# The way down of two ConvFFNs as a Strassen product with the inner tiles in three parts

## The chip, the core and the metric

The kernel runs on one core of one Trainium2 chip. The metric is the device time of one execution in microseconds, taken as the median of several. A core has five engines with queues of their own: TensorE (PE in the rows; PEld is its weight load), VectorE (DVE), ScalarE (ACT), GpSimd (POOL) and SyncE (SP), which here starts the DMA loads. Each engine takes its instructions in order; semaphores tie the engines together.

## The reference

The input is x, 512 positions of 1024 channels in float32. Two layers run one after the other, first a mixer of pooling and block-sparse attention, then a recurrent block, each followed by the same gated ConvFFN with its own weights, and each step adds to the residual:

```python
def conv_ffn(h, w_in, conv_w, conv_b, w_out):
    z = causal_dwconv(h @ w_in, conv_w, conv_b)
    u, g = jnp.split(z, 2, axis=-1)
    return (jax.nn.gelu(g) * u) @ w_out

for l in range(DEPTH):
    x = x + mixer(rms_norm(x, norm_mix[l]))
    x = x + conv_ffn(rms_norm(x, norm_ffn[l]), ...)
```

The inner width is 2816, 22 tiles of 128 channels; `w_in` has 44 such tiles of columns (22 for u, 22 for g), and `w_out` is 2816 x 1024, a product of 22 inner tiles with 8 output tiles.

## The kernel before

Channels lie on partitions and the 512 positions along a row: X[d], d = 0 to 7, are the residual's tiles of 128 x 512. Every product is made of three matmuls (`mm3`, L223 to L226): each float32 operand is split into a high part, a cast that ScalarE makes, and a low part, the rest, that VectorE subtracts. High by high, high by low and low by high are summed in PSUM. A matmul has a 128 x 128 weight tile and up to 512 columns of the moving operand.

All weights come in one list, `chunks`, in the order of use. `load` (L175) starts a chunk's DMA into one of three `wraw` buffers on SP's queue; `convert` (L183) makes `whi` on ScalarE (L195) and `wlo` on VectorE (L196) in one of four pairs of buffers; `wnext` (L199) hands out the next pair and keeps three conversions ahead. A load waits until a `wraw` buffer has been converted, a conversion until TensorE is done with a `whi` and `wlo`.

A ConvFFN (`ffn`) runs in two halves of 11 inner tiles. In the way up of a half, an up tile `up` of g and one of u (24 matmuls each) follow each other; `conv` takes each from PSUM as `z` (VectorE, L700), makes `a` on ScalarE (L702) and adds the two shifted taps on VectorE (L704). g goes through ScalarE's GeLU (`gg`), y = u * gg is VectorE's (L718), and its high and low parts `yy` are kept (L230, L231). In the way down (`down`) each of the 8 output tiles `dn` sums the half's 11 inner tiles (33 matmuls of 512 columns) and VectorE adds it to X[d] (L312). In the last half `after` then makes the next norm's split and sum of squares of X[d] (`Norm.tile_done`: `xh` on ScalarE, `xl` on VectorE, L234, and `ss` on GpSimd, L260), or stores it; the very last tile is done in two halves of 256 columns. The order on each engine is a scheduler's, made when the program is built; where `pe["on"]` is set, TensorE keeps the order of the code.

Of the kernel before, what the change touches and what calls it, by code (L numbers as in the profile page):

```python
# [17 lines left out]
P = 128  # L18
S = 512
# [49 lines left out]

@with_exitstack  # L70
def tile_trunk(ctx: ExitStack, tc: tile.TileContext, xT, par, fpar, w_v, w_q, w_k, w_u, w_pool, w_po, w_ao,
# [63 lines left out]
    chunks = []  # L135
    for src in (w_q, w_k):
        chunks += [(src[i], 1024) for i in range(4)]
    for what in MIX_ORDER:
        if what == "v":
            chunks += [(w_v[i], 1024) for i in range(4)]  # L140
        elif what[0] in "uf":
            chunks.append((w_u[int(what[1])], 1024))
        elif what == "a":
            chunks.append((w_pool, 4 * P))
            chunks += [(w_po[i], 1024) for i in range(4)]
    chunks += [(w_ao[i], 1024) for i in range(4)]

    def ffn_chunks(w_in, w_out):
        for h in range(2):
            for j in range(h * NF // 2, (h + 1) * NF // 2):  # L150
                chunks.extend([(w_in[NF + j], 1024), (w_in[j], 1024)])
            for d in range(KD):
                chunks.extend([(w_out[h][d][:, :6 * P], 6 * P), (w_out[h][d][:, 6 * P:], 5 * P)])

    ffn_chunks(f0_in, f0_out)
    for kind, n in RG_ORDER:
        if kind == "x":
            chunks.append((r_in[RB + n], 1024))
        elif kind == "p":
            if n % 2 == 0:  # L160
                chunks.append((r_ax[n // 2], 4 * P))
        elif kind == "g":
            chunks.append((r_in[n], 1024))
    for d in range(KD):
        chunks.extend([(r_out[d][:, :5 * P], 5 * P), (r_out[d][:, 5 * P:], 5 * P)])
# [16 lines left out]

    def convert():  # L183
        n = chunks[len(ready)][1]
        if len(raws) == len(ready):
            load()
        raw = raws[len(ready)]
# [4 lines left out]
        parts = 2 if len(ready) < 2 else 2 if pe["on"] and len(ready) in FINE else 1  # L192
        for i in range(parts):
            c = slice(i * n // parts, (i + 1) * n // parts)
            nc.scalar.copy(hi[:, c], raw[:, c])  # L195
            nc.vector.tensor_tensor(lo[:, c], raw[:, c], f(hi[:, c]), op=ALU.subtract)  # L196
        ready.append((hi, lo, n))

    def wnext(n, ahead=AHEAD):  # L199
        while len(ready) < min(used[0] + 1 + ahead, len(chunks)):  # L200
            convert()
        hi, lo, got = ready[used[0]]
        assert got == n
        used[0] += 1
        return hi, lo
# [93 lines left out]
    def down(parts, yh, yl, after, cuts=None):  # L299
        nk = len(yh)  # L300
        for d in range(KD):
            w = [wnext(n * P) for n in parts]
            spans = cuts if cuts and d == KD - 1 else [slice(0, S)]
            for t in spans:
                ps = MM("dn")
                k = 0
                for n, (wh, wl) in zip(parts, w):
                    for i in range(n):
                        c = slice(i * P, (i + 1) * P)
                        mm3(ps[:, t], wh[:, c], wl[:, c], yh[k][:, t], yl[k][:, t], k == 0, k == nk - 1)  # L310
                        k += 1
                nc.vector.tensor_tensor(X[d][:, t], ps[:, t], X[d][:, t], op=ALU.add)  # L312
                if len(spans) > 1:
                    after(d, t)
            if len(spans) == 1:
                after(d)
# [376 lines left out]
    def ffn(layer, norm, after, cuts=None):  # L693
# [13 lines left out]
        for h0 in range(2):  # L707
            half(h0 * NF // 2, conv, after if h0 else (lambda d: None), cuts if h0 else None)

    def half(j0, conv, after, cuts):  # L710
        yh, yl = [], []
        for j in range(j0, j0 + NF // 2):
            g = conv(NF + j)
            gg = T("gg")
            nc.scalar.activation(gg, g, AF.Gelu_apprx_tanh)  # L715
            u = conv(j)
            y = T("y")
            nc.vector.tensor_tensor(y, u, gg, op=ALU.mult)  # L718
            hi, lo = split_of(y, None, T("yy", F32R), T("yy", F32R))
# [110 lines left out]
    phase("ffn1", z=4, a=4, gg=2, y=2, yy=30)  # L830
# [4 lines left out]
    ffn(1, nf1, store, [slice(0, S // 2), slice(S // 2, S)])  # L835
# [15 lines left out]
def _two(w):  # L851
    return np.stack([_lhs(w[:FF // 2], KD), _lhs(w[FF // 2:], KD)])
# [11 lines left out]
def _layout(i):  # L864
# [9 lines left out]
    for l in range(2):  # L874
# [32 lines left out]
```

## Time and profile before

| | us |
|---|---|
| three runs, median (lowest to highest) | 1100.43 (1099.63 to 1101.14) |
| the profiled execution | 1099.4 |
| its span, first to last instruction | 1097.6 |
| TensorE busy | 1081.9 |
| VectorE busy | 724.6 |
| ScalarE busy | 514.2 |
| GpSimd busy | 93.1 |

The profile shows one execution. Busy times are sums of an engine's instructions; TensorE's matmuls overlap in a pipeline, so the cost of one is read from the distance of starts and not from its own length. The granted clock of TensorE is given as a share of 2.4 GHz; its mean here is 0.998.

### The profile page before, as it was taken

The page shows a single profiled execution, that of the slowest core. Times are in us where ns is not written, and L with a number is a line of the kernel's source. Part 1 is how long each engine was busy: PE and PEld are TensorE (multiplying, and loading weights), DVE is VectorE, ACT ScalarE, POOL GpSimd, SP SyncE. Part 2 cuts the span into 40 slices and gives each one's busy share as a digit, 9 for nine tenths or more (in the row PEclk, how much of TensorE's full clock was granted, in tenths as well). Part 3 has the DMA queues.
Part 4 walks back from the last instruction along what each step waited for, and adds up shares of the span by engine and source line. Part 5 has one row for each costly group of instructions (what it writes and reads, how often), then busy time and mean ns, then how long its engine had stood idle before and what let it go on. Part 6 is the DMA issues. An engine that isn't in the chain of part 4 may idle for free.

```text
span 1097.6 us, 12782 instructions
## 1 busy us (share of the span) xinstructions
PE 1081.9 (99%) x4895; PEld 891.6 (81%) x4895; DVE 724.6 (66%) x1013; ACT 514.2 (47%) x749; POOL 93.1 (8%) x76
## 2 busy tenths in 40 slices
PE   8999999999999999999999898999999999999998
PEld 6888877888888888888888676888888888888887
DVE  7778877877743577764486969448777435777631
ACT  6557766444422344433448694354444223444420
POOL 5031003000000000001103332120000000000000
PEclk9999999999999999999999999999999999999999
DMA  6332112222233322223323131343332333332241
GB/s 223 131 92 91 58 47 89 97 96 96 67 89 113 116 96 96 84 71 103 118 96 106 48 102 56 102 145 96 96 96 67 91 111 115 96 96 84 78 134 51
DMA packets 35261, 105.40 MB, mean 96 GB/s; under 512 B 4096, under 2 KB 4992, under 8 KB 35200
## 3 DMA queue, kind: packets, MB, share of 16 engines
q1 hardware_dynamic: 34416, 103.48, 29.7%
q10 hardware_dynamic: 784, 1.11, 0.4%
q8 instruction: 38, 0.62, 0.2%
q14 instruction: 23, 0.19, 0.1%
HBM read 101.43 MB, written 2.10 MB: 94 GB/s over the span
## 4 chain that ended last, share of the span: by engine, by line
PE 90%; DVE 6%; ACT 3%; issue 1%; DMA 0%; POOL 0%; SPq 0%; DVEq 0%; ACTq 0%; POOLq 0%
PE up L218 44%; PE dn L218 26%; PE tk L218 5%; PE xr L218 2%; PE gt L218 2%; PE po L218 2%; PE u L218 2%; PE ao L218 2%; DVE h L783 1%; PE gp L218 1%; PE s L218 1%; DVE wlo L196 1%; DVE h L781 1%; PE av L218 1%; PE tr L221 1%
## 5 line engine op out<-in xcount | busy, mean ns | idle before, releaser
L195 ACT CAST whi<-wraw 128x1024 fp32r<-128x1024 f32 (+3 forms) x225 | 202.7, 904 | 278.9 <-PE dn L218 154.2
L196 DVE TENSOR_TENSOR wlo<-wraw,whi 128x1024 fp32r<-128x1024 f32 (+3 forms) x225 | 237.9, 1060 | 112.8 <-ACT whi L195 110.2
L218 PE MATMUL up<-xl,whi 128*128 128x512 f32 x704 | 274.0, 389 | 0.0
L218 PE MATMUL up<-xh,whi 128*128 128x512 f32 x704 | 273.9, 389 | 0.0
L218 PE MATMUL up<-xh,wlo 128*128 128x512 f32 x704 | 273.9, 389 | 0.0
L218 PE MATMUL dn<-yy,whi 128*128 128x512 f32 (+1 forms) x886 | 268.1, 384 | 2.4 <-ACT yy L230 2.0
L218 PEld LDWEIGHTS dn<-yy,whi 128*128 128x128 f32 x886 | 165.0, 188 | 36.7 <-ACT yy L230 2.8
L218 PE MATMUL dn<-yy,wlo 128*128 128x512 f32 (+1 forms) x443 | 170.0, 384 | 0.0
L218 PEld LDWEIGHTS up<-xl,whi 128*128 128x128 f32 x704 | 132.2, 188 | 28.0 <-DVE xl L234 0.5
L218 PEld LDWEIGHTS up<-xh,whi 128*128 128x128 f32 x704 | 132.2, 188 | 27.4
L218 PEld LDWEIGHTS up<-xh,wlo 128*128 128x128 f32 x704 | 132.2, 188 | 27.3
L704 DVE SCALAR_TENSOR_TENSOR a<-z,fprm,a 128x510 f32<-128x510 f32 (+1 forms) x176 | 131.0, 747 | 4.2 <-ACT a L702 0.8
L700 DVE TENSOR_TENSOR z<-up,rbc 128x512 f32<-128x512 f32 x88 | 60.5, 688 | 89.3 <-PE up L218 89.2
L218 PEld LDWEIGHTS dn<-yy,wlo 128*128 128x128 f32 x443 | 83.2, 188 | 16.2
L260 POOL TENSOR_TENSOR ss<-ss,sq 128x512 f32<-128x512 f32 x28 | 40.9, 1462 | 488.3 <-ACT sq L259 487.8
L230 ACT CAST yy<-y 128x512 fp32r<-128x512 f32 x44 | 27.3, 621 | 112.1 <-DVE y L718 112.1
L312 DVE TENSOR_TENSOR x<-dn,x 128x512 f32<-128x512 f32 (+1 forms) x41 | 27.8, 678 | 73.8 <-PE dn L218 73.7
L702 ACT ACTIVATE a<-z,fprm 128x512 f32<-128x512 f32 x88 | 71.4, 813 | 3.8 <-DVE z L700 3.2
L715 ACT ACTIVATE gg<-a 128x512 f32<-128x512 f32 x44 | 27.8, 632 | 80.8 <-DVE a L704 80.8
L231 DVE TENSOR_TENSOR yy<-y,yy 128x512 fp32r<-128x512 f32 x44 | 30.4, 692 | 28.8 <-ACT yy L230 28.8
L218 PE MATMUL tk<-wlo,xh 128*128 128x512 f32 x96 | 37.6, 392 | 2.0 <-DVE wlo L196 2.0
L218 PE MATMUL tk<-whi,xh 128*128 128x512 f32 x96 | 38.0, 401 | 0.5 <-ACT whi L195 0.5
(186 smaller groups left out, 1229.0 us busy)
## 6 DMA issues: line engine op xcount, KB each, us to landing
wraw<-in_dram SPq DMA_DIRECT2D x131, 512.0 KB, 3.3
wraw<-in_dram SPq DMA_DIRECT2D x48, 320.0 KB, 2.9
wraw<-in_dram SPq DMA_DIRECT2D x32, 384.0 KB, 3.1
x<-in_dram SPq DMA_DIRECT2D x8, 256.0 KB, 5.7
out_dram<-x SPq DMA_DIRECT2D x7, 256.0 KB, 2.0
wraw<-in_dram SPq DMA_DIRECT2D x6, 256.0 KB, 2.7
qka<-qka ACTq DMA_DIRECT2D x8, 128.0 KB, 2.3
wraw<-in_dram SPq DMA_DIRECT2D x4, 128.0 KB, 3.4
```

What stands on the lines that cost most here:

```text
L195: nc.scalar.copy(hi[:, c], raw[:, c])
L196: nc.vector.tensor_tensor(lo[:, c], raw[:, c], f(hi[:, c]), op=ALU.subtract)
L218: in_order(nc.tensor.matmul(*a, **k))
L221: in_order(nc.tensor.transpose(*a))
L230: nc.scalar.copy(hi, src)
L231: nc.vector.tensor_sub(lo, src, f(hi))
L260: nc.gpsimd.tensor_tensor(self.ss, self.ss, sq, op=ALU.add)
L312: nc.vector.tensor_tensor(X[d][:, t], ps[:, t], X[d][:, t], op=ALU.add)
L700: nc.vector.tensor_tensor(z, ps, bc, op=ALU.mult)
L702: nc.scalar.activation(a, z, AF.Identity, scale=cw[2], bias=cw[3])
L704: nc.vector.scalar_tensor_tensor(a[:, sh:], z[:, :S - sh], w, a[:, sh:], op0=ALU.mult, op1=ALU.add)
L715: nc.scalar.activation(gg, g, AF.Gelu_apprx_tanh)
```

## The change

Each way down is now a product of blocks by Strassen's scheme in Winograd's form: seven block products take the place of eight. One block is a pair of output tiles (d, d+1) by half of the part's inner tiles by half of the positions (Q = 256). The inner tiles come in three parts, of 8, 8 and 6, in place of two of 11, so a layer has three ways up and three ways down.

On the weights' side of a pair of output tiles stand `a` (the first tile's row of weights, products 1 and 2), `b` (the second half of the second tile's, product 4), `s` (two sums, products 5 and 6) and `r` (two more, products 3 and 7). GpSimd makes `ws` and `wr` by four additions of half a chunk; they are split as other weights are. On the inner side, two inner tiles y give four blocks, and three or four differences `tt` of these (t1, t3, t2, t4) are made by GpSimd, for a part's last two tiles by VectorE; the seven blocks that the products take are split into `yh` and `yl`. Products that share a bank add up in PSUM, and VectorE adds the bank to a half of X[d] behind each product (L816): seven additions of 256 columns for each pair of output tiles and part.

`PORDER` sets the order of products: "10" is product 1 of output pair 0; "20-" leaves out the part's last two inner tiles, which "20+" brings. `WORDER` is the order in which weights are made ready. `pe["on"]` is set in a way down. A product has 12 matmuls in the parts of eight inner tiles and 9 in the part of six.

```diff
+PARTS = ((0, 8), (8, 8), (16, 6))
+Q = S // 2
+QB = {1: 0, 2: 1, 3: 2, 5: 3, 7: 4, 6: 5, 4: 6}
+LEFT = {1: ("a", 0), 2: ("a", 1), 5: ("s", 0), 6: ("s", 1), 3: ("r", 0), 7: ("r", 1), 4: ("b", 0)}
+WORDER = "a0 s0 a1 r0 s1 b0 a2 r1 s2 b1 a3 r2 s3 b2 r3 b3".split()
+BANK = {1: "mm", 6: "mm", 7: "mm", 4: "mm", 5: "s", 3: "s", 2: "tr"}
+PORDER = "10 50 11 20- 21- 20+ 21+ 30 60 51 70 12 40 61 31 22 71 52 41 13 62 32 23 72 53 63 42 73 33 43".split()
...
     def ffn_chunks(w_in, w_out):
-        for h in range(2):
-            for j in range(h * NF // 2, (h + 1) * NF // 2):
-                chunks.extend([(w_in[NF + j], 1024), (w_in[j], 1024)])
-            for d in range(KD):
-                chunks.extend([(w_out[h][d][:, :6 * P], 6 * P), (w_out[h][d][:, 6 * P:], 5 * P)])
+        for j0, n in PARTS:
+            for j in range(j0, j0 + n):
+                plain((w_in[NF + j], 1024), (w_in[j], 1024))
+            base = len(chunks)
+            chunks.extend([(w_out[d][:, j0 * P:(j0 + n) * P], n * P) for d in range(KD)])
+            for k in WORDER:
+                items.append((k[0], base + 2 * int(k[1])))
...
+        if kind == "a":
+            return raw_of(i), n
+        if kind == "b":
+            return raw_of(i + 1)[:, h:], h
+        if kind == "s":
+            a, b = raw_of(i), raw_of(i + 1)
+            s, r = (cur["tp"].tile([P, 1024], F32, name=t, tag=t, bufs=cur["bufs"][t]) for t in ("ws", "wr"))
+            add = nc.gpsimd.tensor_tensor
+            add(s[:, :h], b[:, :h], b[:, h:], op=ALU.add)
+            add(s[:, h:n], s[:, :h], a[:, :h], op=ALU.subtract)
+            add(r[:, :h], a[:, h:], s[:, h:n], op=ALU.subtract)
+            add(r[:, h:n], a[:, :h], b[:, :h], op=ALU.subtract)
...
+            late = i == np_ - 1
+            for k in range(2):
...
+                nc.vector.tensor_tensor(y[:, 2 * k * Q:2 * (k + 1) * Q], u, gg, op=ALU.mult)
+                if k == 0:
+                    cut_of(b[0], 0, 1)
+                    if late:
+                        nc.vector.tensor_tensor(t1, b[1], b[0], op=ALU.subtract)
+                        cut_of(t1, 3, 4)
+            cut_of(y[:, 2 * Q:], 1, 3)
+            if late:
+                nc.vector.tensor_tensor(t3, b[3], b[1], op=ALU.subtract)
+                nc.vector.tensor_tensor(t2, b[3], t1, op=ALU.subtract)
+                nc.vector.tensor_tensor(t4, b[2], t2, op=ALU.subtract)
+                cut_of(t[:, Q:], 4, 7)
+            else:
...
+                nc.gpsimd.tensor_tensor(t2, b[3], t1, op=ALU.subtract)
+                nc.gpsimd.tensor_tensor(t4, b[2], t2, op=ALU.subtract)
+                cut_of(t, 3, 7)
...
+        def add(d, t, ps):
+            nc.vector.tensor_tensor(X[d][:, t], ps[:, :Q], X[d][:, t], op=ALU.add)
...
+            for k in ks:
+                c = slice((half * np_ + k) * P, (half * np_ + k + 1) * P)
+                r = slice(QB[m] * Q, (QB[m] + 1) * Q)
+                mm3(ps[:, :Q], wh[:, c], wl[:, c], yh[k][:, r], yl[k][:, r], m in (1, 5, 2) and k == 0, k == np_ - 1)
...
-    phase("ffn0", z=4, a=4, gg=2, y=2, yy=30)
+    phase("ffn0", z=4, a=4, gg=2, y=2, tt=1, yh=4, yl=4, ws=1, wr=1)
```

The order on two engines shows where the added work stands. On VectorE, before the change, this is the end of the first layer's first way up and the start of its way down (`z` of the last up tile first, then `a`, y, the split `yy` and the first output tile's addition to X):

```order
L700 TENSOR_TENSOR z<-up,rbc 128x512
L196 TENSOR_TENSOR wlo<-wraw,whi 128x640
L704 SCALAR_TENSOR_TENSOR a<-z,fprm,a 128x511
L704 SCALAR_TENSOR_TENSOR a<-z,fprm,a 128x510
L718 TENSOR_TENSOR y<-a,gg 128x512
L231 TENSOR_TENSOR yy<-y,yy 128x512
L196 TENSOR_TENSOR wlo<-wraw,whi 128x768
L312 TENSOR_TENSOR x_71<-dn,x_71 128x512
```

With the change the same place of VectorE's queue, from the `z` of the last up tile on, reads:

```order
L751 TENSOR_TENSOR z<-up,rbc 128x512
L237 TENSOR_TENSOR wlo<-wr,whi 128x1024
L755 SCALAR_TENSOR_TENSOR a<-z,fprm,a 128x511
L816 TENSOR_TENSOR x_71<-dn,x_71 128x256
L755 SCALAR_TENSOR_TENSOR a<-z,fprm,a 128x510
L816 TENSOR_TENSOR x_72<-dn,x_72 128x256
L784 TENSOR_TENSOR y<-a,gg 128x512
L816 TENSOR_TENSOR x_73<-dn,x_73 128x256
L792 TENSOR_TENSOR tt<-y 128x256
L793 TENSOR_TENSOR tt<-y,tt 128x256
L287 TENSOR_TENSOR yl<-y,yh 128x512
```

Between the `z` of the last up tile and the low part of the last y now stand the additions of the products 10, 50 and 11 to X, which wait for TensorE, and two differences; the split in front is that of r0. Behind `yl` come the fourth difference's work, two more additions and the splits of s1 and of the differences.

GpSimd has nothing to do in this place before the change. With it, its queue reads here, from the weights of the first output pair on (`ws` and `wr` of output pair 0, the differences of the third pair of inner tiles, and `ws`, `wr` of output pair 1):

```order
L223 TENSOR_TENSOR ws<-wraw 128x512
L226 TENSOR_TENSOR wr<-wraw 128x512
L224 TENSOR_TENSOR ws<-ws,wraw 128x512
L225 TENSOR_TENSOR wr<-wraw,ws 128x512
L798 TENSOR_TENSOR tt<-y 128x512
L800 TENSOR_TENSOR tt<-y,tt 128x256
L801 TENSOR_TENSOR tt<-y,tt 128x256
L223 TENSOR_TENSOR ws<-wraw 128x512
L224 TENSOR_TENSOR ws<-ws,wraw 128x512
L225 TENSOR_TENSOR wr<-wraw,ws 128x512
L226 TENSOR_TENSOR wr<-wraw 128x512
```

The first nine of these stand where the last four up tiles run, the two for `wr` behind the split of r0, since there is one `wr` buffer. They are followed by four additions for each further output pair, of which the first waits for that pair's second chunk.

## Rows read from the trace of the kernel before

**Rows 1.** The page: busy time of each engine; the chain's shares by line.
```profile
PE 1081.9 (99%) x4895; PEld 891.6 (81%) x4895; DVE 724.6 (66%) x1013; ACT 514.2 (47%) x749; POOL 93.1 (8%) x76
...
PE up L218 44%; PE dn L218 26%; PE tk L218 5%; PE xr L218 2%; PE gt L218 2%; PE po L218 2%; PE u L218 2%; PE ao L218 2%; DVE h L783 1%; PE gp L218 1%; PE s L218 1%; DVE wlo L196 1%; DVE h L781 1%; PE av L218 1%; PE tr L221 1%
```

**Rows 2.** The chain in order of time: start, us, engine, tile, line, instructions.
```profile
306.53 59.84 PE dn L218 x264
...
1034.30 60.28 PE dn L218 x297
```

**Rows 3.** Windows: stretch, us, busy PE PEld DVE ACT POOL, clock, DMA, GB/s.
```profile
306.40:366.40 60.00, 60.00 (x266) 49.71 (x265) 22.98 (x28) 14.82 (x19) 0.00 (x0) 1.00 0.35 105
...
740.50:854.70 114.20, 114.20 (x505) 94.55 (x505) 84.85 (x105) 51.58 (x66) 0.00 (x0) 1.00 0.29 89
```

**Rows 4.** Timeline of TensorE, last output tile: start, us, instruction, count.
```profile
1086.49 0.40 PE L218 MATMUL dn<-yy,whi 128*128 128x256 f32 x2
...
1094.05 0.40 PE L218 MATMUL dn<-yy,whi 128*128 128x256 f32 x2
```

**Rows 5.** Groups by form: busy us, mean ns; idle. Last row: ns minimum/median/maximum.
```profile
L196 DVE TENSOR_TENSOR wlo<-wraw,whi 128x1024 fp32r<-128x1024 f32 x121 | 150.1, 1242 | 40.6 <-ACT whi L195 38.3 <-issue 0.3
...
L195 ACT CAST whi<-wraw 128x1024 fp32r<-128x1024 f32 x121 | 127.2, 1051 | 122.4 <-PE up L218 57.3 <-PE dn L218 29.4 <-issue 12.3
...
L704 DVE SCALAR_TENSOR_TENSOR a<-z,fprm,a 128x511 f32<-128x511 f32 x88 | 65.4, 745 | 1.3 <-ACT a L702 0.8
L700 DVE TENSOR_TENSOR z<-up,rbc 128x512 f32<-128x512 f32 x88 | 60.5, 688 | 89.3 <-PE up L218 89.2
...
L196 DVE TENSOR_TENSOR wlo<-wraw,whi 128x768 fp32r<-128x768 f32 x32 | 30.6, 957 | 62.3 <-ACT whi L195 62.1
...
L231 DVE TENSOR_TENSOR yy<-y,yy 128x512 fp32r<-128x512 f32 x44 | 30.4, 692 | 28.8 <-ACT yy L230 28.8
...
L196 DVE TENSOR_TENSOR wlo<-wraw,whi 128x512 fp32r<-128x512 f32 x22 | 17.1, 799 | 1.1 <-ACT whi L195 1.1
...
L312 DVE TENSOR_TENSOR x<-dn,x x41: 423/691/693, 314.0 to 1094.6; 128x512 f32<-128x512 f32 x39, 128x256 f32<-128x256 f32 x2
```

**Rows 6.** Timeline of VectorE and GpSimd; last row: one line's ns minimum/median/maximum.
```profile
65.11 1.75 DVE L196 TENSOR_TENSOR wlo<-wraw,whi 128x1024 fp32r<-128x1024 f32 x1
...
540.49 0.75 DVE L234 SCALAR_TENSOR_TENSOR xl<-x,prm,xh 128x512 fp32r<-128x512 f32 x1
540.61 1.78 POOL L260 TENSOR_TENSOR ss<-ss,sq 128x512 f32<-128x512 f32 x1 [6.23 <-ACT sq L259]
...
548.58 1.86 DVE L234 SCALAR_TENSOR_TENSOR xl<-x,prm,xh 128x512 fp32r<-128x512 f32 x1
548.61 1.29 POOL L260 TENSOR_TENSOR ss<-ss,sq 128x512 f32<-128x512 f32 x1 [6.22 <-ACT sq L259]
...
622.93 3.13 POOL L824 TENSOR_TENSOR yy<-i,a 128x512 f32<-128x512 f32 x1 [10.48 <-ACT i L820]
...
L797 DVE TENSOR_TENSOR z<-xr,rbc x10: 658/680/691, 556.7 to 635.0; 128x512 f32<-128x512 f32 x10
```

**Rows 7.** Timeline of VectorE at the first layer's first way down.
```profile
306.57 0.69 DVE L700 TENSOR_TENSOR z<-up,rbc 128x512 f32<-128x512 f32 x1 [2.33 <-PE up L218]
...
311.09 0.69 DVE L231 TENSOR_TENSOR yy<-y,yy 128x512 fp32r<-128x512 f32 x1 [0.69 <-ACT yy L230]
```

**Rows 8.** TensorE's waits (total us, times, longest), and windows behind the longest.
```profile
PE gp L218 <- ACT xrs L807: 3.2, 1, 3.2
...
616.00:617.00 1.00, 0.69 (x1) 0.19 (x1) 1.00 (x2) 1.00 (x2) 0.00 (x0) 0.69 0.00 0
617.00:618.00 1.00, 0.79 (x2) 0.69 (x3) 1.00 (x3) 0.98 (x2) 0.00 (x0) 0.50 0.27 59
...
619.00:620.00 1.00, 1.00 (x4) 0.78 (x3) 1.00 (x2) 0.78 (x2) 0.00 (x0) 0.61 0.00 0
```

**Rows 9.** DMA issues: count, KB each, median us to landing.
```profile
wraw<-in_dram SPq DMA_DIRECT2D x131, 512.0 KB, 3.3
```

More of the change, by code (lines that the diff above doesn't have):

```diff
@@ L181, in load, with raw_of, form @@
         raws.append(raw)
-    def convert():
[L184 to L187, printed above, removed]
+    block = {}
+    def raw_of(i):
+        while len(raws) <= i:
+            load()
+        return raws[i]
+    def form(kind, i):
+        n = chunks[i][1]
+        h = n // 2
+        if kind == "a":
[10 more added lines that the diff above has]
+            add(r[:, h:n], a[:, :h], b[:, :h], op=ALU.subtract)
+            block[i] = r
+            return s[:, :n], n
+        return block.pop(i)[:, :n], n
+    def convert():
+        kind, at = items[len(ready)]
+        if kind != "plain":
+            raw, n = form(kind, at)
+            hi, lo = (wp.tile([P, 1024], F32R, name=t, bufs=WB)[:, :n] for t in ("whi", "wlo"))
+            nc.scalar.copy(hi, raw)
+            nc.vector.tensor_tensor(lo, raw, f(hi), op=ALU.subtract)
+            ready.append((hi, lo, n))
+            return
+        n = chunks[at][1]
+        raw = raw_of(at)
         if n == S and "shi" in cur["bufs"]:
@@ L191, in convert @@
             hi, lo = (wp.tile([P, 1024], F32R, name=t, bufs=WB)[:, :n] for t in ("whi", "wlo"))
-        parts = 2 if len(ready) < 2 else 2 if pe["on"] and len(ready) in FINE else 1
+        parts = 2 if len(ready) < 2 else 2 if pe["on"] and "hn" in cur["bufs"] and len(ready) in FINE else 1
         for i in range(parts):
@@ L199, in wnext @@
     def wnext(n, ahead=AHEAD):
-        while len(ready) < min(used[0] + 1 + ahead, len(chunks)):
+        while len(ready) < min(used[0] + 1 + ahead, len(items)):
             convert()
         hi, lo, got = ready[used[0]]
+        used[0] += 1
+        if n is None:
+            return hi, lo, got
         assert got == n
-        used[0] += 1
         return hi, lo
@@ L297, in up_tile, with down @@
         return ps
-    def down(parts, yh, yl, after, cuts=None):
+    def down(parts, yh, yl, after):
         nk = len(yh)
@@ L690, in tile_trunk, with ffn @@
     ring[:] = ["mm", "s", "mm", "s", "mm", "av"]
-    def ffn(layer, norm, after, cuts=None):
+    def ffn(layer, norm, after, cut=False):
         def conv(m):
@@ L705, in conv @@
             return a
-        for h0 in range(2):
-            half(h0 * NF // 2, conv, after if h0 else (lambda d: None), cuts if h0 else None)
-    def half(j0, conv, after, cuts):
-        yh, yl = [], []
[L712 to L719, printed above, removed]
+        for i, (j0, n) in enumerate(PARTS):
+            part(j0, n, conv, after if i == len(PARTS) - 1 else None, cut)
```

114 lines of the change are left out of this document (82 added, 32 removed).

## The prediction

> **What bounds the kernel now.** I read the page's busy shares first: TensorE is busy for 99% of the span, VectorE for 66%, ScalarE for 47%, GpSimd for 8%, and the chain that ended last has 44% of the span in matmuls of the way up (`up`) and 26% in those of the way down (`dn`) [rows 1]. So time is saved only by giving TensorE less to do, and lost by any wait put in front of it. The chain in order of time then shows the four ways down, one for each half of the inner tiles in each layer: three take 59.84 us for 264 matmuls (one stands in the rows), the last 60.28 us for 297, since its last tile is done in two column halves [rows 2]. The windows show what stands beside TensorE: in a way up VectorE works 84.85 of 114.2 us, ScalarE 51.58, GpSimd nothing; in a way down VectorE 22.98 of 60 us, GpSimd nothing; TensorE is busy throughout in both [rows 3].
>
> **The matmuls removed.** A matmul of 512 columns costs 59.84/264 = 0.2267 us of TensorE. The change's matmuls have 256 columns, and the trace has 66 of these: they start at 1086.49 and the last three at 1094.05, so 63 matmuls in 7.56 us, 0.120 us each [rows 4]. That is not half of 0.2267: each matmul has about 13 ns that do not shrink. Per layer the new way down has 7 products x 4 pairs of output tiles x 11 pairs of inner tiles x 3 passes = 924 matmuls, 924 x 0.120 = 110.9 us. The four old stretches sum to 59.84 x 3 + 60.28 = 239.8 us, the new ones to 221.8: 18.0 us less. An eighth of the products goes, but only 7.5% of the time. The Trainium skill, TensorE: Matmul & The Clock Gate, section Back-to-back issue gap, puts the gap at N/2.4 + 2.5 ns. That would make the prices 216 and 109 ns and the gain about 26 us by estimate; the rows are 11 ns above it at both widths, and the sum goes by the rows.
>
> **What VectorE, ScalarE and GpSimd get.** The prices are those of [rows 5]. Per pair of output tiles in a part of eight inner tiles: three splits of 1024 columns and one of 512 (two chunks of weights used to take two of 1024) and seven additions to X for two, on VectorE 3 x 1.24 + 0.80, and 7 x 0.42 (the last row's 256-column form) = 7.5 us beside 84 x 0.120 = 10.1 us of matmuls. In the part of six it is 3 x 0.96 + 0.56 (my estimate for 384 columns from the 256- to 512-column rows) + 2.9 = 6.4 of 7.6 us. ScalarE has 3 x 1.05 + 0.62 = 3.8 us. Neither bounds by itself. GpSimd gets four additions of 512 columns, at the 1.29 us that the bare ones take [rows 6] = 5.2 us; in the way up three subtractions per pair of inner tiles, about 2.6 us if 256 columns cost half of 512 (not shown; between 0.5 and 1.29 each).
>
> **The port.** These two engines do not work independently. In [rows 6] VectorE's `xl` (two SBUF inputs) takes 0.75 us alone and 1.86 us when GpSimd's `ss` starts beside it; elsewhere `ss` takes 1.78 us for its 1.29 when `xl` is first. A `wlo` of 1024 columns takes 1.75 us at 65.11, among GpSimd's pooling sums, and at 622.93 one GpSimd multiplication takes 3.13 us while VectorE runs one operation into the next. VectorE's operations with one input in PSUM are not held: the ten z of the recurrent block, where GpSimd works, all take 658 to 691 ns. So each GpSimd operation of 512 columns can cost VectorE 1.86 - 0.75 = 1.11 us, or wait itself. The Trainium skill says the same in SBUF — State Buffer, section SBUF: two separate sides: the shared port pair is an exclusive lock against a VectorE instruction with two SBUF inputs, and the loser fully blocks. By that rule nothing of GpSimd's work is free beside such instructions; the trace agrees (1.86 for 0.75 us).
>
> **The seam from way up to way down.** T is the start of the first product. TensorE first needs the last inner tile's low part at the second matmul of `20+`: after 12 + 12 + 12 + 9 + 9 + 1 = 55 matmuls, T + 6.6 us (T + 4.8 us in the part of six, 40 matmuls). Before, the eleventh inner tile came last in the accumulation, at 306.4 + 30 x 0.2267, and its `yy` was ready at 311.78: no wait [rows 7]. Now the VectorE queue of that chain also holds a split and three additions. With z ending at T + 0.86 (as in [rows 7], 307.26 with T at 306.4): ScalarE's `whi` at T + 1.05, `wlo` of r 1.24, then a 0.75, x 0.42, a 0.75, x 0.42, y 0.69, x 0.42, two differences 0.42, `yl` 0.69: T + 7.3 us, a wait of 0.7 us (2.1 us in the part of six, where `wlo` and the differences end at about T + 6.9). That is the floor, with GpSimd not felt.
>
> With the port: in the four up tiles ahead of T (4 x 5.44 = 21.8 us) VectorE's own work is four `wlo` 5.0, four z 2.8, eight a 6.0, two y 1.4 (each as `yy`), four splits of y and its differences 2.8 and one difference 0.4 = 18.3 us, 3.5 us free. GpSimd has, by the order, four additions for s0 and r0, three subtractions, two additions for s1: 6 x 1.11 + 2.2 = 8.9 us of port. If what is free and the z's (2.8) take their share, VectorE is 2.6 us late at T; if none can be used (a VectorE that waits for ScalarE is late anyway), 8.9. The two additions for r1 come behind T: 2.2 less what lies beside the three x (1.3) = 0.9. So the wait is 0.7 + 2.6 + 0.9 = 4.2 us, between 0.7 and 11.8. For the part of six the same sum with 0.83 us per 384-column addition (estimate, three quarters) and 4.3 us free, three `wlo` being shorter, gives 7.2 - 4.3 - 2.8 = 0.1, and 1.7 - 1.3 = 0.4: 2.6 us, between 2.1 and 11. I take 4.2 and 2.6: 4 x 4.2 + 2 x 2.6 = 22.0 us. Behind the late `yl` stand `wlo` of s1 and the split of the other differences, which product `60` needs: 0.35 us more, x 6 = 2.1.
>
> **The clock.** The only long TensorE wait of the trace (3.2 us, `gp` for `xrs`) is followed by a granted clock of 0.69, 0.50 and, two windows on, 0.61 [rows 8]. Taken as 0.50, the 1.2 GHz level, from about 616.4 to 619.8, that is some 3 us at half speed, 1.5 us lost. I charge it once in each part of eight, 6 us, none in the parts of six; the bounds are 0 and 9.
>
> **The last pair's weights.** `13` needs a3. Its load waits for a raw buffer that the additions for r2 free; these wait for s2, that for the load of b2, that for the split of b0. From the start of `12`: b2 landed at +0.9, four additions, then the landing, 3.3 us for 512 KB [rows 9], `whi` 1.05, `wlo` 1.24: ready at +11.9 without the port and +15.4 with each addition and split in turn; TensorE is there at 8 x 1.44 + 0.24 = +11.8. Waits of 0.25 to 3.6 us, 1.9 taken; in the part of six the same chain gives 1.2 to 4.1, 2.65 taken. Sum 4 x 1.9 + 2 x 2.65 = 12.9 us.
>
> **At nothing.** The bytes of w_out are the same, in 24 loads per layer for 32; DMA is not on the chain now. Three parts make one more return to the way up per layer: the first up weights find a buffer four products ahead, behind `63`. The last two output tiles now end 1.1 us apart (nine matmuls) instead of 7.5 (33 of the wide ones), so the norm's splits bunch up; the first `xr` tile's 24 matmuls, 5.4 us, cover them, and without that cover they cost up to two `ss`, 2.6 us, once.
>
> **The sum.** Waits 22.0 + 2.1 + 6 + 12.9 = 43 us. The profiled execution took 1099.4 us (span 1097.6 and 1.8 outside it), the median is 1100.43, 1.0 above. 1099.4 - 18.0 + 43 + 1.0 = 1125 us, 2.3% slower.
>
> **The rivals.** *Faster:* GpSimd's additions lose the port and still come in time, so that VectorE is not held. The 3.13 us row speaks for it, and in a way up VectorE is free a quarter of the time; against it, 1.86 and 1.75 are VectorE's losses. Then the floors remain: 4 x 0.7 + 2 x 2.1 + 2.1 + 4 x 0.25 + 2 x 1.2 = 12.5 us, 1100.4 - 18.0 + 12.5 = 1095 us. It decides at 3.0 us of waits per part (18.0/6). *The same:* waits of about 3 us per part eat the gain, 1100 us. *Far slower:* every GpSimd operation holds VectorE for its full time and the low clock follows each seam: 4 x 11.8 + 2 x 11 + 9 + 2.1 + 4 x 3.6 + 2 x 4.1 = 103 us, 1185 us; VectorE's quarter of free time speaks against it.
>
> **How the numbers follow.** This kernel's runs spread by 0.14%, so 0.2% (2.2 us) is about what can be told from no change. Chances: my forecast with the waits between its bounds 0.68, and in it 1104 to 1160; faster, 0.22, 1086 to 1098; the same, 0.10. Leaving out about 0.08 at each end, the range is 1092 to 1160.
>
> **What would show it.** Right: `dn` matmuls 0.120 us apart; waits of TensorE at `dn` for `yl`, `yh` and `wlo` in each of six parts; GpSimd's `ws` and `wr` well above 1.29 us or VectorE's `wlo` and a above their 1.24 and 0.75; a granted clock below 1.00 behind the seams. Wrong: six ways down of about 40 and 30 us with hardly a wait, or `wlo` and a at their old means while GpSimd runs.

## The result and the profile after

The changed kernel takes 1184.42 us, the median of four runs (1183.63 to 1184.63), beside 1100.79 us for the kernel before: a ratio of 1.0758, 95% interval 1.0740 to 1.0777. It is 83.6 us slower. The forecast was slower, 1125 us, with a range up to 1160; the sign was right and the size was not. The time is that of the rival called far slower, 1185 us.

The page of the profiled execution (span 1182.8 us, for 1097.6) answers to [rows 1]. First the busy times, then the shares of the chain that ended last, by engine.

```profile
PE 1096.5 (93%) x5654; PEld 936.2 (79%) x5654; DVE 889.6 (75%) x1232; ACT 555.7 (47%) x809; POOL 314.6 (27%) x220
...
PE 40%; DVE 28%; POOL 12%; ACT 10%; DMA 5%; issue 4%; SPq 0%; ACTq 0%; POOLq 0%; DVEq 0%
```

TensorE had 90% of the chain before and has 40% now; VectorE and GpSimd together have 40%. The windows of the six ways down (stretch, us, busy time of PE, PEld, DVE, ACT and POOL with instructions, granted clock, DMA share, GB/s) answer to [rows 3]:

```profile
275.02:330.65 55.63, 44.02 (x337) 42.51 (x336) 42.11 (x61) 19.93 (x24) 20.54 (x12) 0.94 0.24 77
417.72:473.70 55.98, 45.27 (x337) 43.98 (x336) 42.33 (x61) 19.93 (x24) 20.85 (x12) 0.91 0.24 77
539.01:586.98 47.97, 33.99 (x244) 32.30 (x243) 40.17 (x61) 22.58 (x35) 19.88 (x14) 0.89 0.23 66
868.75:924.39 55.64, 44.10 (x338) 42.59 (x336) 42.13 (x61) 19.93 (x24) 20.38 (x12) 0.94 0.25 78
1011.45:1068.39 56.94, 46.95 (x338) 45.65 (x337) 43.30 (x61) 20.02 (x24) 19.54 (x12) 0.88 0.24 76
1133.69:1179.65 45.96, 35.94 (x253) 34.59 (x251) 32.73 (x57) 14.20 (x21) 13.24 (x10) 0.85 0.22 72
```

They sum to 318.1 us, 319.2 with the nine matmuls of the third that come a little later; the four before summed to 239.8. So the ways down lose 79.4 us of the span's 85.2. The rest is small: 2.8 us between the first layer's last way down and the recurrent block's, 1.7 us in that, and 1.3 us ahead of the first way up. TensorE's part of one way down (its timeline: start, us, instruction, and in brackets the idle time before it with what ended it):

```profile
278.51 0.39 PE L274 MATMUL dn<-yh,whi 128*128 128x256 f32 x1 [2.27 <-ACT yh L286]
...
279.20 0.28 PE L274 MATMUL dn<-yh,wlo 128*128 128x256 f32 x1
...
280.88 0.28 PE L274 MATMUL dn<-yl,whi 128*128 128x256 f32 x1
...
290.20 0.58 PE L274 MATMUL dn<-yh,whi 128*128 128x256 f32 x1 [5.40 <-ACT yh L286]
291.15 0.58 PE L274 MATMUL dn<-yl,whi 128*128 128x256 f32 x1 [0.37 <-DVE yl L287]
...
307.44 0.39 PE L274 MATMUL dn<-yh,whi 128*128 128x256 f32 x1 [0.81 <-DVE x L816]
...
313.23 0.36 PE L274 MATMUL dn<-yh,whi 128*128 128x256 f32 x1 [2.65 <-DVE x L816]
```

Between waits the matmuls start 0.120 us apart (14 in the 1.68 us from 279.20 to 280.88), as [rows 4] had it. There are two places of waiting: the seam, for the last inner tiles' splits, 8.0 us, and later, ahead of `71` and `41`, for an addition to X, 3.5 us. Behind the long wait the granted clock is 0.50, the 1.2 GHz level (a window of TensorE alone):

```profile
292.00:294.00 2.00, 2.00 (x11) 0.50 0.01 2
```

The table of TensorE's waits (total us, times, longest) shows both over all six:

```profile
PE dn L274 <- ACT yh L286: 41.0, 10, 6.1
PE dn L274 <- DVE x L816: 23.5, 13, 3.5
...
PE dn L274 <- DVE yl L287: 1.8, 6, 0.4
```

What delays the splits is seen one way up earlier. These are VectorE, GpSimd and ScalarE in the last four up tiles ahead of the second way down, which begins at 417.72:

```profile
399.04 1.84 POOL L223 TENSOR_TENSOR ws<-wraw 128x512 f32<-128x512 f32 x1 [15.21 <-DMA wraw<-in_dram]
399.65 3.48 DVE L755 SCALAR_TENSOR_TENSOR a<-z,fprm,a 128x511 f32<-128x511 f32 x2
...
400.85 1.74 POOL L226 TENSOR_TENSOR wr<-wraw 128x512 f32<-128x512 f32 x1
402.54 1.75 POOL L224 TENSOR_TENSOR ws<-ws,wraw 128x512 f32<-128x512 f32 x1
403.16 1.67 DVE L784 TENSOR_TENSOR y<-a,gg 128x512 f32<-128x512 f32 x1
404.36 1.63 POOL L225 TENSOR_TENSOR wr<-wraw,ws 128x512 f32<-128x512 f32 x1
...
405.95 1.74 POOL L798 TENSOR_TENSOR tt<-y 128x512 f32<-128x512 f32 x1
...
407.06 1.72 DVE L237 TENSOR_TENSOR wlo<-wraw,whi 128x1024 fp32r<-128x1024 f32 x1
407.77 1.59 POOL L800 TENSOR_TENSOR tt<-y,tt 128x256 f32<-128x256 f32 x1
409.44 0.74 POOL L801 TENSOR_TENSOR tt<-y,tt 128x256 f32<-128x256 f32 x1
410.21 1.05 ACT L286 CAST yh<-tt 128x1024 fp32r<-128x1024 f32 x1 [3.78 <-POOL tt L801]
...
411.30 1.23 DVE L287 TENSOR_TENSOR yl<-tt,yh 128x1024 fp32r<-128x1024 f32 x1 [2.53 <-ACT yh L286]
```

The two engines take strict turns. Two a, 1.5 us in [rows 5], take 3.48; a y takes 1.67 for 0.69; a `wlo` 1.72 for 1.24; and the GpSimd sums, 1.29 bare in [rows 6], take 1.6 to 1.8. From 408.78 to 411.30 VectorE, late as it is, does nothing: its next split waits for ScalarE, and ScalarE for the differences that GpSimd, held as long itself, has ready only at 410.18. VectorE's z, which reads one of its inputs from PSUM, isn't held: one starts at 406.45, in the middle of a GpSimd operation (405.95 to 407.69), and no z of the ConvFFNs takes more than 692 ns. The y of the kernel before (busy us, mean ns), then the z of the changed kernel (ns minimum/median/maximum):

```profile
L718 DVE TENSOR_TENSOR y<-a,gg 128x512 f32<-128x512 f32 x44 | 30.4, 692 | 1.4
```

```profile
L751 DVE TENSOR_TENSOR z<-up,rbc x88: 676/685/692, 198.4 to 1138.2; 128x512 f32<-128x512 f32 x88
```

In the first way down the same lateness is read from one row each of VectorE's timeline: its last z starts at 282.50, 7.5 us behind the way down's start at 275.02, and `yl` of the last inner tile at 290.42.

The second place is in the way down itself, at 304 to 313 us (GpSimd, SP's queue, ScalarE, VectorE):

```profile
304.22 2.28 POOL L226 TENSOR_TENSOR wr<-wraw 128x512 f32<-128x512 f32 x1
...
306.53 0.88 SPq L201 DMA_DIRECT2D wraw<-in_dram  x2
...
310.45 1.04 ACT L236 CAST whi<-wraw 128x1024 fp32r<-128x1024 f32 x1 [5.96 <-DMA wraw<-in_dram]
...
311.53 1.23 DVE L237 TENSOR_TENSOR wlo<-wraw,whi 128x1024 fp32r<-128x1024 f32 x1 [3.28 <-ACT whi L236]
...
312.67 0.42 DVE L816 TENSOR_TENSOR x<-dn,x 128x256 f32<-128x256 f32 x1
```

The last sum ends at 306.50 and frees a raw buffer; the load goes out at 306.53; its split holds VectorE's queue until 312.7; and behind it stands the addition to X that reads the bank (VectorE's row at 312.67). The product at 313.23, `41`, adds on in that bank and waits for it.

### The profile page after: what moved, and what is told of

Its sections match the earlier page's. It is cut to its first block, busy times and chain, and to the rows that moved or that the text cites. A ratio compares the mean times of both kernels' runs of the same rounds, so it can differ in the third digit from the quotient of the medians.

```text
span 1182.8 us, 14821 instructions
## 1 busy us (share of the span) xinstructions
PE 1096.5 (93%) x5654; PEld 936.2 (79%) x5654; DVE 889.6 (75%) x1232; ACT 555.7 (47%) x809; POOL 314.6 (27%) x220
## 4 chain that ended last, share of the span: by engine, by line
PE 40%; DVE 28%; POOL 12%; ACT 10%; DMA 5%; issue 4%; SPq 0%; ACTq 0%; POOLq 0%; DVEq 0%
PE dn L274 14%; PE up L274 9%; DVE a L755 8%; DVE wlo L250 5%; DMA wraw<-in_dram 4%; PE tk L274 3%; DVE wlo L237 3%; PE xr L274 3%; ACT whi L249 3%; DVE y L784 3%; PE gt L274 2%; DVE yl L287 2%; ACT yh L286 2%; POOL tt L798 2%; PE po L274 2%
## 5 line engine op out<-in xcount | busy, mean ns | idle before, releaser
L274 PE MATMUL dn<-yh,whi 128*128 128x256 f32 x616 | 186.2, 302 | 65.5 <-ACT yh L286 41.0
L250 DVE TENSOR_TENSOR wlo<-wraw,whi 128x1024 fp32r<-128x1024 f32 (+3 forms) x161 | 183.0, 1141 | 52.6 <-ACT whi L249 51.6
L249 ACT CAST whi<-wraw 128x1024 fp32r<-128x1024 f32 (+3 forms) x161 | 151.7, 948 | 119.2 <-PE up L274 37.9
L274 PE MATMUL dn<-yl,whi 128*128 128x256 f32 x616 | 184.4, 299 | 2.1 <-DVE yl L287 1.8
L274 PEld LDWEIGHTS dn<-yh,whi 128*128 128x128 f32 x616 | 126.9, 206 | 70.7 <-ACT yh L286 43.0
L274 PE MATMUL dn<-yh,wlo 128*128 128x256 f32 x616 | 182.5, 296 | 0.3
L274 PEld LDWEIGHTS dn<-yl,whi 128*128 128x128 f32 x616 | 126.8, 206 | 5.2 <-DVE yl L287 4.8
L274 PEld LDWEIGHTS dn<-yh,wlo 128*128 128x128 f32 x616 | 126.7, 206 | 1.1 <-DVE wlo L237 1.1
L223 POOL TENSOR_TENSOR ws<-wraw 128x512 f32<-128x512 f32 (+1 forms) x24 | 40.5, 1689 | 218.9 <-DMA wraw<-in_dram 133.1
L286 ACT CAST yh<-y 128x256 fp32r<-128x256 f32 (+1 forms) x44 | 22.6, 513 | 151.3 <-DVE y L784 151.3
L816 DVE TENSOR_TENSOR x<-dn,x 128x256 f32<-128x256 f32 x168 | 68.9, 419 | 24.4 <-PE dn L274 23.2
```

Source lines behind the costliest of these rows:

```text
L223: add(s[:, :h], b[:, :h], b[:, h:], op=ALU.add)
L274: in_order(nc.tensor.matmul(*a, **k))
L286: nc.scalar.copy(hi, src)
L816: nc.vector.tensor_tensor(X[d][:, t], ps[:, :Q], X[d][:, t], op=ALU.add)
```

## The experiments

The theory, A: GpSimd's sums and VectorE's operations with two SBUF inputs exclude each other, VectorE is late ahead of each seam for that, and nearly all the loss is this. The rival, B: the order of the queues does it; a third engine now stands between load and split, and every hop delays an in-order queue, whatever the operations cost. Against both stands a third: the low clock behind the waits.

**No GpSimd work.** `s` and `r` hand on the raw chunks and the differences are left out; products, splits and loads stay.

```diff
-            add(s[:, :h], b[:, :h], b[:, h:], op=ALU.add)
...
-            return s[:, :n], n
+            return raw_of(i), n
...
-                cut_of(t, 3, 7)
+                cut_of(y, 3, 7)
```

> Left out: every GpSimd operation of the ConvFFNs (s and r hand on the raw chunks, the split of the four differences reads the four blocks of y instead), so all products, loads, splits and buffers stay and the sums are missing. Theory A (GpSimd and VectorE hold each other, and VectorE is late at every seam because of it): the waits fall to the floors of the prediction, 12.5 us, so 1100 - 18 + 12 = 1095 us, bounds 1086 and 1105. Theory B (the queues' order does it: VectorE's row of splits behind the last up product is long whoever adds): the seam waits of 8 and 7 us stay, only those at a3 go, so 1184 - 6 x 3.5 = 1163 us, not under 1140.

1105.33 us, ratio 1.0033 (1.0021 to 1.0044). 79 us of the loss go with 144 GpSimd operations, 0.3 us past theory A's upper bound (1105) and far under theory B's 1140. But the 1095 of the floors isn't met either. Its largest waits (total us, times, longest) are for weights:

```profile
PE dn L267 <- DVE wlo L230: 5.0, 8, 0.8
...
PE dn L267 <- ACT whi L229: 3.0, 6, 0.7
```

**Weight sums left out, and differences left out.** Each of the two edits above alone.

> Left out: GpSimd's four additions per pair of output tiles (s and r hand on raw chunks); its differences of y stay. 96 of the 144 GpSimd operations of the two layers go, and with them the waits at a3. Theory A: seams keep three held differences of the pair before the last, some 3 us late: about 1110 us (1095 to 1130). Theory B: as without any GpSimd work, 1163 us.

1120.78 us, ratio 1.0176 (1.0159 to 1.0192).

> Left out: GpSimd's three differences per inner pair (the split reads the four blocks of y instead); the weight additions stay. Theory A: the additions are the larger part of what holds VectorE, six of nine operations ahead of a seam: about 1155 us (1130 to 1170). Theory B: 1180 us, since the queues are as before.

1163.79 us, ratio 1.0562 (1.0546 to 1.0578). Above the kernel without either, the differences alone cost 15.5 us and the weight sums alone 58.5; together they cost 79.1, so they add up with only 5 us more. Per operation that is 0.32 us for each of the 48 differences and 0.61 us for each of the 96 sums. Both times lie within theory A's bounds (1095 to 1130 and 1130 to 1170).

**All on VectorE.** The full computation.

```diff
-            add = nc.gpsimd.tensor_tensor
+            add = nc.vector.tensor_tensor
...
-                nc.gpsimd.tensor_tensor(t2, b[3], t1, op=ALU.subtract)
+                nc.vector.tensor_tensor(t2, b[3], t1, op=ALU.subtract)
```

> The full computation; every GpSimd operation of the ConvFFNs is put on VectorE at the same place of the program. VectorE's own work grows by some 144 x 0.6 = 86 us, and it is never held. Theory A: VectorE has 3.5 us free in the 21.8 us ahead of a seam and gets 9 operations of 0.42 to 0.75 us, 5.5 us, where the port cost it up to 8.9: less late than before, 1115 to 1150 us. Theory B, and any theory by which the amount of VectorE's work decides: at or above 1184 us.

1121.03 us, ratio 1.0168 (1.0151 to 1.0185): 63 us of the loss come back by giving a busier engine more work. A 512-column sum takes 0.69 us on VectorE. The 144 operations cost 15.7 us above no work at all, 0.11 us each, where they cost 0.55 each on GpSimd (79.1/144).

**Hops without work.** To part excluded time from hops, every GpSimd operation was kept with its place and its followers but cut to 16 columns. The sums are left out. First in place:

```diff
-            add(s[:, :h], b[:, :h], b[:, h:], op=ALU.add)
+            w = 16
+            add(b[:, :w], b[:, :w], b[:, h:h + w], op=ALU.add)
```

> Every GpSimd operation is kept with its place in the queue, its inputs and its followers, but does 16 columns (in place, on the chunk or block that is split next), so the sums are left out, and the hops from engine to engine stay. Theory A (the time in which GpSimd and VectorE exclude each other is the cost): near the 1105.3 us of the kernel without GpSimd, 1104 to 1113. Theory B (the cost is that splits, and behind them TensorE, wait for a third engine in order): some six hops of 1 us or more per part stay, 1130 to 1160 us.

1148.76 us, ratio 1.0425 (1.0398 to 1.0451), which would be theory B's. But writing in place gave GpSimd waits that the changed kernel lacks: it now stands behind VectorE's splits of the same block (GpSimd's waits: total us, times, longest).

```profile
POOL y L797 <- DVE yl L286: 238.2, 16, 26.8
```

So the run was repeated with tiles that stand through the phase:

```diff
-            s, r = (cur["tp"].tile([P, 1024], F32, name=t, tag=t, bufs=cur["bufs"][t]) for t in ("ws", "wr"))
-            add(s[:, :h], b[:, :h], b[:, h:], op=ALU.add)
+            s, r = keep["ws"], keep["wr"]
+            add(s[:, :16], b[:, :16], b[:, h:h + 16], op=ALU.add)
```

> Again 16 columns for each GpSimd operation of the ConvFFNs, now into tiles of their own that stand through the phase (set once at its start), so that every split waits for the same sums and blocks as in the changed kernel and GpSimd waits for no split that it does not wait for there; the sums are left out. Theory A (the excluded time is the cost): 1105 to 1115 us. Theory B (hops): 1130 to 1160 us. In the first run with 16 columns GpSimd waited for the splits of the blocks that it wrote in place, 238 us at y, and its 1149 us can come from that; if this one also stays near 1149, the order of the queues costs that much by itself.

1098.66 us, ratio 0.9977 (0.9968 to 0.9987). All hops of the changed kernel are in it and cost nothing; theory B falls. It is also under the kernel without GpSimd work by 6.7 us, and the waits for `wlo` that stand there are gone. The likeliest reason, argued and not tried, is that there `s` and `r` hold the raw buffers until their splits. A part of eight, and the part of six with a norm behind it:

```profile
401.72:442.67 40.95, 40.74 (x338) 40.50 (x336) 31.45 (x52) 17.02 (x19) 3.44 (x10) 1.00 0.36 105
507.98:543.22 35.24, 31.04 (x244) 29.59 (x243) 32.28 (x54) 19.96 (x30) 10.40 (x14) 1.00 0.31 90
```

**Work without waiting.** Every sum is done in full but into tiles that nobody reads, so no split waits for GpSimd; the sums are left out of the result.

```diff
-            block[i] = r
-            return s[:, :n], n
-        return block.pop(i)[:, :n], n
+            return a, n
+        return raw_of(i + 1), n
```

> Every GpSimd operation is done in full, on the same inputs at the same place, but its result goes to a tile that nobody reads: the splits read the raw chunks and the blocks of y, so no split waits for GpSimd; only a raw buffer and a block of y come free later. Theory A: VectorE is held as before, ws and wr take 1.6 to 1.7 us on average, and the waits at the seams stay: 1150 to 1180 us. Theory B: 1105 to 1115 us, since nothing waits for a sum. Between them, 1120 to 1145, would be a cost shared by both.

1161.74 us, ratio 1.0550 (1.0533 to 1.0568). 56.4 us of the 79.1 are lost though nobody waits for a sum: VectorE is held. It is busy for 906.8 us with the same 1232 instructions that take 833.1 without GpSimd (busy times without GpSimd's work, then of this run):

```profile
PE 1074.2 (97%) x5654; PEld 917.0 (83%) x5654; DVE 833.1 (76%) x1232; ACT 557.7 (51%) x809; POOL 94.2 (9%) x76
```

```profile
PE 1089.1 (94%) x5654; PEld 929.0 (80%) x5654; DVE 906.8 (78%) x1232; ACT 556.4 (48%) x809; POOL 323.1 (28%) x220
```

Raw buffers and blocks of y come free later in this run too; the run with sums far ahead of the seam, below, reads no raw buffer and loses 44.0 us with 96 additions. The other 22.7 us come with waiting for sums that are themselves held (the row of 3.78 us above); that share is argued from the difference.

**The clock.** Extra matmuls fill the waits at the seam, 44 and 16 of them into a free bank.

```diff
+            if what == "20+":
+                fill(44)
...
+                if what == "10" and k == 3:
+                    fill(16)
```

> The changed kernel, full computation, with small extra matmuls into a bank that is free there: 44 (4.7 us) ahead of the last inner pair of product 20, where TensorE waits 5.4 and 6.1 us, and 16 (1.7 us) ahead of that of product 10 in the parts of eight, where it waits 2.3. They fill a wait and delay nothing. If the half clock behind the seam (0.50 for some 5 us, 2.5 us lost) is lost time, 1184 - 6 x 2 = 1172 us, bounds 1166 and 1178. If VectorE sets the pace there and TensorE at full clock only waits longer at the next place, 1182 to 1186.

1184.44 us, ratio 1.0750 (1.0734 to 1.0766): nothing gained. The stretch behind the seam now has the full clock, and TensorE waits longer at the next place, 1.91 us where it was 0.81 (windows, then TensorE's timeline):

```profile
288.65:297.00 8.35, 7.98 (x60) 7.42 (x61) 7.69 (x15) 3.81 (x5) 0.00 (x0) 1.00 0.36 116
...
305.66 0.39 PE L274 MATMUL dn<-yh,whi 128*128 128x256 f32 x1 [1.91 <-DVE x L822]
```

So most of the half clock at the seam is a mark of the loss, not a term of it. In the parts of eight TensorE reaches `41` only 0.1 to 0.6 us earlier, counted from the first product, for the 2 us expected: the addition that it waits for ends a chain of late splits, loads and sums that the filling doesn't touch. That little is lost again behind this wait, where the clock now falls in three of the four parts of eight, in the changed kernel in one (the twelve products from `41` on, first part, first the changed kernel):

```profile
313.23 17.59 PE dn L274 x144
```

```profile
311.12 19.08 PE dn L274 x144
```

Filling the later waits wasn't tried.

**Three parts alone.** Plain products of 512 columns in parts of 8, 8 and 6 inner tiles.

```diff
+        down((n,), yh, yl, after or (lambda d: None), [slice(0, S // 2), slice(S // 2, S)] if cut and after else None)
```

> The division into three parts (8, 8, 6) alone: plain way down of 512 columns in each part, no block products, no sums. By the prediction the third return to the way up costs nothing: 1100 to 1102 us. If the third seam itself costs (two more additions to X per output tile, one more start of the up weights per layer), 1104 us or more, and then a part of what the kernel without GpSimd loses against its TensorE sum is not the block products' at all.

1102.77 us, ratio 1.0012 (1.0003 to 1.0021): 1.5 us above the kernel before, measured beside it at 1101.3, which is less than the 0.2% that the prediction takes as the least that can be told. A plain way down of eight inner tiles takes 43.87 to 43.89 us, so the block products without port cost give 2.9 us in each part of eight (40.95).

**The same work beside plain products.** To that kernel 144 unused sums and differences were added, on GpSimd, in the same stretches; the computation stays full.

```diff
             nc.scalar.copy(hi[:, c], raw[:, c])
+            if at in summed:
+                add(s[:, :h], b[:, :h], b[:, h:], op=ALU.add)
+                add(s[:, h:n], s[:, :h], raw[:, :h], op=ALU.subtract)
+                add(r[:, :h], raw[:, h:], s[:, h:n], op=ALU.subtract)
+                add(r[:, h:n], raw[:, :h], b[:, :h], op=ALU.subtract)
```

> The kernel of three plain parts (1102.8 us), and beside it the same number of GpSimd sums and differences in the same stretches, full size, into tiles that nobody reads. If GpSimd's operations cost by themselves wherever they run beside VectorE, some 50 us as with the block products: 1140 to 1165. If they cost only where VectorE's row of work ahead of a TensorE need is already full, as at the new seams: 1103 to 1112, since here VectorE has some 37 of 60 us free in a way down and the last split is needed 30 matmuls into it.

1154.39 us, ratio 1.0490 (1.0469 to 1.0510). Of the two expectations the first holds. VectorE has 26% of its time free in a way up and the last split is needed only 30 matmuls into the way down, and still the work costs 51.6 us. TensorE waits at the seam again, six times; the seventh wait of the row, 2.0 us, is the recurrent block's and stands in the kernel before too (total us, times, longest):

```profile
PE dn L282 <- ACT yy L294: 40.8, 7, 8.1
```

**The same work far ahead of the seam.** 16 unused additions in each part, all in its first four inner tiles, beside the plain products:

```diff
+            if j - j0 < 4:
+                for k in range(4):
+                    nc.gpsimd.tensor_tensor(t[:, k * S:(k + 1) * S], y, gg, op=ALU.add)
```

> The kernel of three plain parts (1102.8 us) with 16 unused GpSimd additions of 512 columns in each part, as many as its weight sums in the kernel with unused sums (1154.4 us; its differences of y are left out here), but in the first four inner tiles of each way up, two or more inner tiles (22 us) ahead of the seam. If VectorE's free time absorbs what GpSimd holds when there is time until the seam: 1102 to 1107 us. If work held once is lost wherever it is: 1135 to 1150 us.

1146.74 us, ratio 1.0408 (1.0391 to 1.0425): 44.0 us for 96 additions, 0.46 us each, so the place hardly helps. The last quarter of a way up tells why. First the plain kernel of three parts, then this one, which has no GpSimd work there any more but is late:

```profile
382.40:404.13 21.73, 21.73 (x97) 18.00 (x96) 15.90 (x20) 9.77 (x13) 0.00 (x0) 1.00 0.33 98
```

```profile
392.10:413.89 21.79, 21.79 (x98) 18.02 (x96) 17.13 (x23) 10.39 (x14) 0.00 (x0) 1.00 0.41 122
```

VectorE works 17.13 us for 15.90 and still idles 4.7 us. Of 5.8 us that look free it uses 1.2 to catch up; 4.3 of the rest are waits for ScalarE, which makes the high half of each split first (`wlo` for `whi` 2.2 us, `yy` for `yy` 2.1 us). This late row of work wasn't run faster than its hand-overs allow.

**Memsets and copies.** As the kernel with unused sums, with GpSimd's sums replaced by whole-tile memsets behind 16 columns of each sum, and by copies of the same columns (the memsets' edit):

```diff
-            add(s[:, :h], b[:, :h], b[:, h:], op=ALU.add)
+            for _ in range(2):
+                nc.gpsimd.memset(s, 0.01)
```

> As the kernel with unused sums (1161.7 us), with GpSimd's long operations replaced: 16 columns of the sum, then whole-tile memsets, which read nothing, for a like time. If GpSimd holds VectorE by any work on SBUF, 1140 to 1165 us and VectorE's splits and additions stay above their bare times. If only its operations that read two tiles hold it, 1105 to 1112 us with VectorE's at their bare times.

> As the kernel with unused sums (1161.7 us), with every GpSimd sum replaced by a copy of the same columns, which reads one tile. If any GpSimd reading of SBUF holds VectorE: some 1140 to 1162 us by its shorter time, and VectorE's splits and additions above their bare times. If only two read operands do: 1105 to 1112 us, like the memsets (1106.9 us).

1106.87 us, ratio 1.0053 (1.0037 to 1.0069), and 1106.68 us, ratio 1.0056 (1.0037 to 1.0074), both within 1.6 us of no GpSimd work. The groups of the memsets first, one of GpSimd and one of VectorE (busy us, mean ns), then the copies:

```profile
L227 POOL MEMSET wr<- 128x1024 f32 x48 | 45.8, 953 | 0.0
...
L237 DVE TENSOR_TENSOR wlo<-wraw,whi 128x1024 fp32r<-128x1024 f32 x48 | 58.1, 1224 | 10.2 <-ACT whi L236 10.0
```

```profile
L226 POOL COPY wr<-wraw 128x512 f32<-128x512 f32 x16 | 18.8, 1173 | 0.0
...
L796 POOL COPY tt<-y 128x512 f32<-128x512 f32 x16 | 9.9, 616 | 248.4 <-DVE y L783 248.4
...
L236 DVE TENSOR_TENSOR wlo<-wraw,whi 128x1024 fp32r<-128x1024 f32 x48 | 61.1, 1286 | 15.4 <-ACT whi L235 15.3
```

137 us of memsets hold VectorE by nothing (834.1 us busy for 833.1). The copies do hold it (846.6), and are held (1173 ns for 616), but they are half as long, and that much VectorE still absorbs. So my second expectation was right in the time and wrong in the reason: an operation that reads one tile does exclude VectorE. The Trainium skill has this rule in SBUF — State Buffer, section SBUF: two separate sides: a VectorE instruction with two SBUF inputs locks out only a GpSimd operation that reads SBUF, and the loser blocks fully. The two runs agree with it: VectorE's split of 1024 columns takes 1224 ns beside memsets, as without GpSimd's work (1223), and 1286 beside copies.

**Sums for r later, on VectorE.** An attempt at a better full version.

```diff
-            block[i] = r
+            block[i] = r, s
             return s[:, :n], n
+        r, s = block.pop(i)
+        add(r[:, :h], a[:, h:], s[:, h:n], op=ALU.subtract)
+        add(r[:, h:n], a[:, :h], b[:, :h], op=ALU.subtract)
```

> As the kernel with all sums on VectorE (1121.0 us, full computation), but the two sums for r are queued where r is split, not with those for s, so that never more than two sums and one split stand ahead of an addition to X. If the waits for additions to X queued behind four sums (14.0 us there) are the rest of its loss, 1108 to 1114 us; if VectorE's amount of work is (37 of 45 us in a way down), 1119 to 1123.

1121.43 us, ratio 1.0188 (1.0169 to 1.0207): no gain over 1121.03, as expected if the amount of VectorE's work decides. That it does is argued: the waits for additions to X are gone, and TensorE waits for the splits of weights in their place (`whi` 8.1 us, `wlo` 4.1). No version with the full computation beat the kernel before, and the one with sums that cost nothing beat it by 0.23%.

## Why the prediction was wrong

**The matmuls removed: right.** 0.120 us per matmul, and 40.95 us for a part of eight where nothing holds it, 40.3 by the sum.

**The floors: nearly right.** The sum gave 1095 us if GpSimd costs nothing; it is 1098.66. In the run with 16 columns product `20` doesn't wait in a part of eight, where the sum had 0.7 us, and `60` waits 0.2; all waits of the ways down sum to 7.4 us for 12.5. Against these 5.1 us stand 4.6 us above matmuls and waits in the ways down and 5.7 us outside them, both put at nothing.

**The port: the mechanism was right.** GpSimd's work costs 1184.4 - 1098.7 = 85.8 us, the whole of the loss and 2.2 us more. One reading didn't bear its weight: none of the ten z named as not held runs beside a GpSimd operation (those of that stretch stand at 572.40, 579.15 and so on, between the z). The statement holds; the changed kernel's z show it.

**The seam wait: here the sum failed.** The step is "If what is free and the z's (2.8) take their share, VectorE is 2.6 us late at T; if none can be used (a VectorE that waits for ScalarE is late anyway), 8.9." I took 2.6. VectorE's last z starts 7.5 us behind T, for 0.2 us where GpSimd's work is gone: 7.3 us late. Most of the free time isn't there to be used, since it lies between VectorE's hand-overs with ScalarE; the sentence named that reason, and I left it at the far end. The run with early sums shows it by itself, 1.2 of 5.8 us used. Behind T came 2.3 us more, not 0.9 (`yl` at T + 15.4, the z at T + 7.5, against 5.8 and 0.2). The waits of all six seams sum to 41.0 + 1.8 = 42.8 us for 22.0, all within the bounds given. Part of the wait, 2.2 to 2.5 us in each part of eight, stands where the sum didn't look: ahead of the last inner pair of product `10`, nine matmuls behind T. The 2.1 us at product `60` didn't appear.

**The clock: mis-sized as a term.** The ways down last 319.2 us; without 67.3 us of waits 251.9 remain, 30 us above the 221.8 of their matmuls, for restarts behind waits and half clock, and 6 were charged for the clock. In the run with 16 columns the same difference is 4.6 us, so the half clock and the restarts behind the longer waits take some 25. But little of that time at the seam can be got back, as the filled waits show. How the rest divides between clock and restarts stays open.

**The last pair's weights: the place nearly right, the way not.** In the parts of eight TensorE waits ahead of `41`, the product before `13`, and not for a3 itself, but for an addition to X that stands behind a3's late split in VectorE's queue. 23.5 + 1.0 = 24.5 us for 12.9, with 0.6 to 0.8 us in each part of eight at `71`, two products earlier; the bounds summed to 22.6. Queueing behind the waiting instruction was left out of that step. Its sum was also off by a little: the terms named for +11.9 add up to 11.65.

**At nothing.** Outside the ways down 5.8 us are lost. The norm's bunched splits cost 2.8 us between the layers, the 2.6 us that I gave as the price without cover. The cover, one `xr` tile, was too short: `bc` behind it waits 1.05 and 0.54 us.

**The chance.** Far slower was dismissed because of "VectorE's quarter of free time". That is the same failed step. That its 1185 us were met is luck: it had 69.2 us of waits at the seams, where 42.8 were measured, and 9 for the clock, where clock and restarts took 30.

**The account.** By the sum the profiled execution would have taken 1099.4 - 18.0 + 43 = 1124.4 us; it took 1184.6. The 60.2 us between are 20.8 at the seams, 24.1 of clock and restarts, 11.6 at the last pair and 5.8 outside the ways down, less the 2.1 for `60`.

## What to carry to other kernels

Before work is handed to GpSimd, count what it reads: beside a VectorE that mostly runs two-input SBUF operations, a GpSimd sum costs the chain a good part of its own time. Here 144 of them cost 0.55 us each above the kernel without them and 0.60 above the one with 16 columns, while on VectorE itself the same operations cost 0.11 and 0.16 us each, and memsets hardly anything. An engine's idle share is a poor reserve when its row of work alternates with another engine's; ask what the gaps wait for before they are spent. And a half clock behind a wait can be a mark of the loss: fill the wait to see whether it is a cost.

## What was not expected of the hardware

A GpSimd subtraction of 256 columns takes 0.74 us where VectorE stands still (the row at 409.44, with VectorE idle from 408.78 to 411.30), where 512 columns take 1.29. It is seldom that short: half of this line's subtractions take 1.65 us, more than a bare one of twice the width (ns minimum/median/maximum).

```profile
L801 POOL TENSOR_TENSOR tt<-y,tt x16: 736/1654/1657, 216.9 to 1123.4; 128x256 f32<-128x256 f32 x16
```

In the recurrent block, whose code is the same in both kernels, TensorE waits 1.97 us for `yy` before and 1.98 after. Before, the clock stays at 1.00 and the way down takes 57.87 us; after, it falls, and the matmuls of 512 columns stand 0.43 us apart for some 3 us:

```profile
721.67:781.20 59.53, 57.11 (x241) 46.05 (x240) 31.25 (x42) 26.70 (x39) 8.27 (x6) 0.97 0.38 113
```

The same wait is followed by a low clock in one kernel and not in the other; the rows don't show what decides it.
